# A two-layer decoder trunk: twelve instead of nine of 22 feed-forward groups in seven-product form, in a written order, with the weight sums kept in the loaded tiles

## The chip, the core and the metric

The kernel runs on one core of one Trainium2 chip. The metric is the device time of one execution in microseconds (us); less is better. The engines are named as in the profile: PE is TensorE (matmuls; PEld its weight loads), DVE is VectorE, ACT is ScalarE, POOL is GpSimd, SP is SyncE, which only issues DMAs here.

## What is computed

One sequence of 256 tokens with 2048 features passes a gated DeltaNet layer and an HGRN2 layer, each followed by a SwiGLU feed-forward part; all in float32.

```python
def swiglu(h, w_gate, w_up, w_down):
    return (jax.nn.silu(h @ w_gate) * (h @ w_up)) @ w_down

for layer in range(2):
    h = h + mixer[layer](rmsnorm(h, mixer_norm[layer]))
    h = h + swiglu(rmsnorm(h, ffn_norm[layer]), w_gate[layer], w_up[layer], w_down[layer])
return rmsnorm(h, final_norm)
```

w_gate and w_up are 2048 x 5632, w_down is 5632 x 2048. The change touches only the gate and up products of the two feed-forward parts.

## The kernel before

Every large weight is streamed once from HBM. The stream is a list of **items** (`stream`, L634). An item is one 128 x 1024 piece of a weight (512 KB). It is loaded by a DMA from SP's queue into a tile `raw` (a ring of four), then split in two: ACT copies it, rounded to fp32r, into `wh`, and DVE writes `wl` = raw - wh. Both have four buffers (SPLIT_BUFS). PE then makes three fp32r products in the place of one fp32 product: x_high with wh, x_high with wl, x_low with wh. So the split of an item can begin only when PE has finished the item four places before it, and a wl that comes late holds PE up.

The recording layer keeps the matmuls of the items in the order of the list. All other instructions are placed by a planner (`plan`, L319) with a table of costs and due times; it writes each engine's queue in a fixed order, and each engine executes its queue in that order. In the profile all instructions carry line 501, where the recorded queue is issued, so groups are told apart by the names of their tiles.

A feed-forward part has 22 **groups**, each of 256 gate and 256 up columns, and the `down` products in four parts that follow the groups 0-5, 6-11, 12-17 and 18-21. A group exists in two forms:

- plain (`gate_up`): eight items, each of 12 matmuls with 512 columns, all into one PSUM tile `main` (two of these, two banks each). ACT and DVE then make silu(gate) * up in two halves (`gated`).
- seven-product (`mixed_group`): the tokens, the contraction and the columns are halved, and seven products of half-size blocks replace eight (Strassen's scheme as Winograd wrote it). The sums of the activations are made once for each feed-forward part (`mix_inputs`, tiles `mixh`, `mixl`). The weights are taken in four **steps** (kk = 0 to 3). Each step loads two pieces, (b11, b12) and (b21, b22), into tiles `sraw` (a ring of four), and makes four items of them: b11 alone (product 1), then b21 and b22 (products 2 and 3), and two items of sums that DVE adds first, with two adds of 512 elements in each: (b11+b12, b22+b12) for products 5 and 7, and (b22+b11+b12, b22+b11+b12+b21) for products 6 and 4. The sums get `sraw` buffers of their own, so one step takes all four buffers. A step has 42 matmuls with 256 columns. The seven products lie in four PSUM banks, the `aux` tiles: 1 and 2 in the first, 3 and 7 in the second, 5 and 6 in the third, 4 in the fourth. There are only four `aux` banks, so the next such group begins when `end` has read the banks: ACT copies product 1 (`p1`), DVE makes v = product 6 - p1, then p1 + product 2, and so on through six more instructions.

FF_PLAN writes the order of the list. In "6 7 9 : 8 down 10 11 : 0000202..." the items of the seven-product groups 6, 7 and 9 are woven into those of groups 8, the waiting `down` part, 10 and 11: behind the k-th of these follow as many seven-product items as the k-th digit says.

Of the kernel before, what the change touches and what calls it, by code (L numbers as in the profile page):

```python
# [17 lines left out]
P = 128  # L18
T = 256
# [4 lines left out]
N_FF = 22  # L24
FF_PARTS = (6, 6, 6, 4)
FF_PLAN = (
# [4 lines left out]
)  # L31
N_HGRN = 4
LEVELS = (64, 32, 16, 8, 4, 2, 1)
# [491 lines left out]
class Trunk:  # L525
# [359 lines left out]
    def ffn(self, j, after):  # L885
# [68 lines left out]
        def mixed_group(gi):  # L954

            banks, raws = [], {}
# [21 lines left out]
            def raw_ring():  # L978
                return self.tile(self.pool, [P, 1024], "sraw", bufs=4, ordered=True)

            def add(out, x, y):
                nc.vector.tensor_tensor(out=out, in0=x, in1=y, op=ALU.add)

            def keep(half):
                def pre(raw):
                    raws[half] = quarters(raw)
                return pre

            def sums(which):
                def pre(t):  # L990
                    t = t.rearrange("p (n k c) -> p n k c", n=2, k=2)
                    (b11, b12), (b21, b22) = ([q[:, i] for i in range(2)] for q in (raws[0], raws[1]))
# [7 lines left out]
                return pre  # L1000

            def item(kk, src, pre, parts, part=None):
# [44 lines left out]
            for kk in range(4):  # L1047
                halves = [gu[gi, (kk + 4 * h) // 2][:, kk % 2 * 1024 : (kk % 2 + 1) * 1024] for h in range(2)]
                items += [
                    item(kk, halves[0], keep(0), [(1, lambda k: k * 512)], lambda x: quarters(x)[:, 0]),  # L1050
                    item(kk, halves[1], keep(1), [(2, lambda k: k * 512), (3, lambda k: k * 512 + T)]),
                    item(kk, None, sums(0), [(5, lambda k: k * T), (7, lambda k: 512 + k * T)]),
                    item(kk, None, sums(1), [(6, lambda k: k * T), (4, lambda k: 512 + k * T)]),
                ]
            items[0].begin, items[-1].end = begin, end
            return items
# [970 lines left out]
```

## Time and profile before

| what | value |
|---|---|
| time, median of 3 runs (lowest to highest) | 2727.85 us (2725.13 to 2728.78) |
| the profiled execution: its time, its span | 2727.04 us, 2725.3 us |
| PE, DVE, ACT busy, share of the span | 99 %, 78 %, 58 % |
| matmuls of seven-product groups, first and last | 870.0 to 1458.5 us, 2059.5 to 2648.0 us |
| HBM traffic over the span | 220 GB/s |

The profile shows one execution. Its page gives busy times by engine, the span in 40 slices, the chain of work that ended last, and the costliest groups of instructions; further views of the same trace give a timeline of single instructions, busy times in chosen windows, and who waited for whom. A row "out<-in" names the tile that is written and those that are read, with the buffer numbers left out. Two things have to be kept apart in it: the length of an instruction's row, and the time from its start to the start of the next one on the same engine, which can be less.

### The profile page before, as it was taken

Reading aid. Unit: us, or ns where it says so; the run is one execution under the profiler, and the core shown is the slowest. Engines: PE = TensorE matmul, PEld = TensorE weight load, DVE = VectorE, ACT = ScalarE, POOL = GpSimd, SP = SyncE. Lnnn points to the kernel's source line nnn. Section 1 sums busy time; section 2 is a strip of 40 time slices with the busy share of each in tenths; the row PEclk is TensorE's granted clock in tenths of the full one; section 3 lists DMA queues with packets and bytes.
Section 4 is the critical chain, followed back from the end, with each engine's and each line's share of the span. In section 5 each row is a group of like instructions: output and inputs, shape, how many; then the busy total and the mean of one; then the engine's idle time right before and its main releaser. Section 6 shows DMA issues by size and latency. Waiting matters only on the chain.

```text
span 2725.3 us, 44609 instructions
## 1 busy us (share of the span) xinstructions
PE 2707.2 (99%) x16966; PEld 2354.3 (86%) x16966; DVE 2129.8 (78%) x3221; ACT 1591.7 (58%) x2246; POOL 325.2 (12%) x466
## 2 busy tenths in 40 slices
PE   9999999999999999999999999999999999999998
PEld 9888888888888888888888989989888888888886
DVE  6887888787659778788788688678578788878786
ACT  7647676765555555565555656556465555555554
POOL 1222223222110000000000100000100000000010
PEclk9999999999999999999999999999999999999999
DMA  8686667687786677767777655545776777677775
GB/s 276 203 270 207 206 214 239 218 254 203 225 250 211 218 229 228 240 213 236 243 221 223 229 167 178 175 158 182 200 259 210 227 221 235 222 224 232 231 231 194
DMA packets 173959, 599.64 MB, mean 220 GB/s; under 512 B 21674, under 2 KB 22842, under 8 KB 173616
## 3 DMA queue, kind: packets, MB, share of 16 engines
q1 hardware_dynamic: 138912, 503.15, 55.8%
q0 software_dynamic: 34544, 92.79, 13.5%
q8 instruction: 133, 2.18, 0.3%
q10 hardware_dynamic: 288, 0.85, 0.1%
q14 instruction: 82, 0.67, 0.1%
HBM read 550.52 MB, written 48.28 MB: 220 GB/s over the span
## 4 chain that ended last, share of the span: by engine, by line
PE 97%; DVE 1%; ACT 1%; DMA 1%; issue 0%; SPq 0%; POOLq 0%; POOL 0%; ACTq 0%; DVEq 0%
PE main L501 78%; PE aux L501 19%; DVE turned L501 0%; ACT dec L501 0%; DVE wl L501 0%; DMA raw<-in_ffn_gu 0%; DMA first<-in_x 0%; ACT wh L501 0%; ACT xt_h L501 0%; ACT junk L501 0%; DVE htl L501 0%; DVE h L501 0%; SPq L501 0%; DVE p L501 0%; ACT mixh L501 0%
## 5 line engine op out<-in xcount | busy, mean ns | idle before, releaser
L501 ACT ACTIVATE wh<-raw 128x1024 fp32r<-128x1024 f32 x801 | 846.8, 1060 | 842.5 <-PE main L501 720.0
L501 DVE TENSOR_TENSOR wl<-raw,wh 128x1024 fp32r<-128x1024 f32 x801 | 982.7, 1229 | 421.2 <-ACT wh L501 413.5
L501 PE MATMUL main<-wl,xt_h 128*128 128x512 f32 x1600 | 626.8, 392 | 1.9 <-DVE wl L501 1.9
L501 PE MATMUL main<-wh,xt_h 128*128 128x512 f32 x1600 | 625.9, 391 | 1.2 <-ACT wh L501 1.2
L501 PE MATMUL main<-wh,xt_l 128*128 128x512 f32 x1600 | 625.7, 391 | 0.0
L501 DVE TENSOR_TENSOR wl<-sraw,wh 128x1024 fp32r<-128x1024 f32 (+1 forms) x288 | 308.0, 1087 | 65.9 <-ACT wh L501 64.8
L501 ACT ACTIVATE wh<-sraw 128x1024 fp32r<-128x1024 f32 (+1 forms) x288 | 271.8, 949 | 148.0 <-PE main L501 77.6
L501 PEld LDWEIGHTS main<-wh,xt_l 128*128 128x128 f32 x1600 | 300.7, 188 | 62.3
L501 PEld LDWEIGHTS main<-wl,xt_h 128*128 128x128 f32 x1600 | 300.6, 188 | 61.5 <-DVE wl L501 2.5
L501 PEld LDWEIGHTS main<-wh,xt_h 128*128 128x128 f32 x1600 | 300.5, 188 | 61.6 <-ACT wh L501 2.1
L501 PE MATMUL main<-xt_h,wh 128*128 128x256 f32 (+1 forms) x1040 | 289.1, 278 | 0.0
L501 PE MATMUL main<-xt_l,wh 128*128 128x256 f32 (+1 forms) x1040 | 288.5, 277 | 0.6 <-DVE xt_l L501 0.6
L501 PE MATMUL main<-xt_h,wl 128*128 128x256 f32 (+1 forms) x1040 | 288.0, 277 | 0.0
L501 PE MATMUL main<-wh,hth 128*128 128x512 f32 x688 | 268.9, 391 | 0.6 <-ACT hth L501 0.6
L501 PE MATMUL main<-wl,hth 128*128 128x512 f32 x688 | 268.9, 391 | 0.1
L501 PE MATMUL main<-wh,htl 128*128 128x512 f32 x688 | 268.1, 390 | 0.2
L501 PE MATMUL aux<-wl,mixh 128*128 128x256 f32 x864 | 239.2, 277 | 0.0
L501 PE MATMUL aux<-wh,mixh 128*128 128x256 f32 x864 | 239.2, 277 | 0.0
L501 PE MATMUL aux<-wh,mixl 128*128 128x256 f32 x864 | 239.1, 277 | 0.0
L501 PEld LDWEIGHTS main<-xt_l,wh 128*128 128x128 f32 (+1 forms) x1040 | 194.4, 187 | 1.3 <-DVE xt_l L501 0.8
L501 PEld LDWEIGHTS main<-xt_h,wh 128*128 128x128 f32 (+1 forms) x1040 | 194.4, 187 | 0.9
L501 PEld LDWEIGHTS main<-xt_h,wl 128*128 128x128 f32 (+1 forms) x1040 | 194.4, 187 | 0.0
(241 smaller groups left out, 3948.7 us busy)
## 6 DMA issues: line engine op xcount, KB each, us to landing
raw<-in_ffn_gu SPq DMA_DIRECT2D x208, 512.0 KB, 4.7
raw<-in_ffn_d SPq DMA_DIRECT2D x176, 512.0 KB, 4.8
sraw<-in_ffn_gu SPq DMA_DIRECT2D x144, 512.0 KB, 5.7
raw<-in_hgrn_in SPq DMA_DIRECT2D x128, 512.0 KB, 4.3
raw<-in_gdn_kq SPq DMA_DIRECT2D x64, 512.0 KB, 5.3
raw<-in_gdn_v SPq DMA_DIRECT2D x64, 512.0 KB, 4.5
raw<-in_gdn_z SPq DMA_DIRECT2D x64, 512.0 KB, 5.2
raw<-in_gdn_out SPq DMA_DIRECT2D x64, 512.0 KB, 5.3
```

The lines of the kernel that those rows point to most:

```text
L501: getattr(getattr(tc.nc, op.eng), op.method)(*args, **kw)
```

## The change

Twelve groups instead of nine take the seven-product form in each of the two feed-forward parts: groups 4, 11 and 17 are new. The order is written anew: a digit may now be 1 to 6, where it was 0 or 2. And the weight sums are written over the loaded pieces: b11+b12 over b11, b22+b12 over b12, b22+b11+b12 over b22, and the last sum over b21. So a step takes two of the four `sraw` buffers instead of all four, and the first add has to come behind the split of the first item, which reads b11.

```diff
-    "0 | 2 : 1 3 4 5 : 00000002002002002002002002002000",
-    "6 7 9 : 8 down 10 11 : 000020202202022020220202202022020220202202020000",
...
+    "0 | 2 4 : 1 3 5 : 000222022222022222022200",
+    "6 7 9 11 : 8 down 10 : 0213230124002250412010350050110402060002",
...
-                    if which == 0:
-                        raws[2] = t[:, 0]
-                        add(t[:, 0], b11, b12)
-                        add(t[:, 1], b22, b12)
-                    else:
-                        add(t[:, 0], b22, raws[2])
-                        add(t[:, 1], t[:, 0], b21)
+                    if which == 0:
+                        add(b11, b11, b12)
+                        add(b12, b22, b12)
+                    else:
+                        add(b22, b22, b11)
+                        add(b21, b22, b21)
...
-                return Item(src, mm, pre, ring=raw_ring, part=part)
+                return Item(src, mm, pre, ring=lambda: raws[half] if src is None else raw_ring(half), part=part)
...
-                    item(kk, None, sums(0), [(5, lambda k: k * T), (7, lambda k: 512 + k * T)]),
-                    item(kk, None, sums(1), [(6, lambda k: k * T), (4, lambda k: 512 + k * T)]),
+                    item(kk, None, 0, sums(0), [(5, lambda k: k * 512), (7, lambda k: k * 512 + T)]),
+                    item(kk, None, 1, sums(1), [(6, lambda k: k * 512 + T), (4, lambda k: k * 512)]),
```

**The first place is the change from group 6 to group 7** in the first feed-forward part. On PE stand, before, the last matmuls of group 6 (tile aux_1555, product 4) and what follows them, a `down` item:

```order
L501 MATMUL aux_1554_10217<-wl_1636_10598,mixh_1316_8895 128x256
L501 MATMUL aux_1554_10217<-wh_1635_10587,mixl_1317_8896 128x256
L501 MATMUL aux_1555_10241<-wh_1635_10587,mixh_1316_8895 128x256
L501 MATMUL aux_1555_10241<-wl_1636_10598,mixh_1316_8895 128x256
L501 MATMUL aux_1555_10241<-wh_1635_10587,mixl_1317_8896 128x256
L501 MATMUL main_1624_10535<-wh_1638_10605,hth_1515_8891 128x512
```

Two such items of 12 matmuls (5138 to 5161 in PE's order) lie there between the two groups. In the changed kernel group 7 follows group 6 at once, with product 1 in aux_1635:

```order
L501 MATMUL aux_1559_10261<-wh_1618_10584,mixh_1316_8895 128x256
L501 MATMUL aux_1559_10261<-wl_1619_10601,mixh_1316_8895 128x256
L501 MATMUL aux_1559_10261<-wh_1618_10584,mixl_1317_8896 128x256
L501 MATMUL aux_1560_10306<-wh_1618_10584,mixh_1316_8895 128x256
L501 MATMUL aux_1560_10306<-wl_1619_10601,mixh_1316_8895 128x256
L501 MATMUL aux_1560_10306<-wh_1618_10584,mixl_1317_8896 128x256
L501 MATMUL aux_1635_10649<-wh_1621_10596,xt_h0_12_68 128x256
L501 MATMUL aux_1635_10649<-wl_1622_10614,xt_h0_12_68 128x256
```

DVE's order at the same place, before: `p4` is v, and the row that reads aux_1552 is the last reader of group 6's first bank.

```order
L501 TENSOR_TENSOR wl_1642_10644<-raw_1640_10510,wh_1641_10627 128x1024
L501 TENSOR_TENSOR p4_1644_10658<-aux_1554_10217,p1_1643_10583 128x256
L501 SCALAR_TENSOR_TENSOR p1_1643_10583<-aux_1552_10147,rstd_3_59,p1_1643_10583 128x256
L501 TENSOR_TENSOR wl_1651_10669<-sraw_1649_10528,wh_1650_10646 128x2x256
L501 TENSOR_TENSOR sg_1646_10675<-aux_1554_10217,p4_1644_10658 128x256
L501 TENSOR_TENSOR wl_1654_10681<-sraw_1652_10550,wh_1653_10661 128x1024
L501 TENSOR_TENSOR h1_1645_10688<-aux_1553_10161,sg_1646_10675 128x2x256
L501 TENSOR_TENSOR p4_1644_10658<-aux_1553_10161,p4_1644_10658 128x256
L501 SCALAR_TENSOR_TENSOR p4_1644_10658<-aux_1555_10241,rstd_3_59,p4_1644_10658 128x256
```

And in the changed kernel, from the split of group 6's last item (wl_1619); aux_1557 is group 6's first bank:

```order
L501 TENSOR_TENSOR wl_1619_10601<-sraw_1609_10365,wh_1618_10584 128x1024
L501 TENSOR_TENSOR wl_1622_10614<-sraw_1620_10435,wh_1621_10596 128x2x256
L501 TENSOR_TENSOR sraw_1620_10435<-sraw_1620_10435 128x2x256
L501 TENSOR_TENSOR wl_1625_10632<-sraw_1623_10492,wh_1624_10609 128x1024
L501 TENSOR_TENSOR p4_1627_10642<-aux_1559_10261,p1_1626_10592 128x256
L501 SCALAR_TENSOR_TENSOR p1_1626_10592<-aux_1557_10209,rstd_3_59,p1_1626_10592 128x256
L501 TENSOR_TENSOR sg_1629_10647<-aux_1559_10261,p4_1627_10642 128x256
L501 TENSOR_TENSOR p4_1627_10642<-aux_1558_10225,p4_1627_10642 128x256
L501 TENSOR_TENSOR h1_1628_10657<-aux_1558_10225,sg_1629_10647 128x2x256
L501 TENSOR_TENSOR wl_1634_10666<-raw_1632_10464,wh_1633_10628 128x1024
```

What moved: the plain items between the two groups are gone, and five reads of the banks stand in one run, with three rows between them and the split of the last item. Groups 13 and 15 meet in the same way, so there are two such places in each feed-forward part. At six others one plain item (four places) or two (two places) lie between.

**The second place is where the first seven-product group begins**, group 2. DVE's order there before (wl_1372 is the split of its first item; turned, h1 and mixl belong to `mix_inputs`):

```order
L501 TENSOR_TENSOR h1_1325_9209<-turned_1323_9108,h1_1324_9176 128x512
L501 TENSOR_TENSOR mixl_1317_8896<-h1_1324_9176,mixh_1316_8895 128x512
L501 TENSOR_TENSOR wl_1372_9222<-sraw_1370_8883,wh_1371_9211 128x2x256
L501 TENSOR_TENSOR mixl_1317_8896<-h1_1324_9176,mixh_1316_8895 128x512
L501 TENSOR_TENSOR mixl_1317_8896<-h1_1325_9209,mixh_1316_8895 128x512
L501 SCALAR_TENSOR_TENSOR h1_1348_9238<-main_1326_8900,rstd_3_59,sg_1349_8881 128x256
L501 SCALAR_TENSOR_TENSOR h1_1348_9238<-main_1326_8900,rstd_3_59,sg_1350_8882 128x256
L501 TENSOR_TENSOR h1_1325_9209<-turned_1322_9090 128x512
L501 TENSOR_TENSOR wl_1375_9249<-sraw_1373_8884,wh_1374_9235 128x1024
L501 TENSOR_TENSOR mixl_1317_8896<-h1_1325_9209,mixh_1316_8895 128x512
L501 TENSOR_TENSOR wl_1385_9267<-raw_1383_9154,wh_1384_9256 128x1024
L501 TENSOR_TENSOR wl_1392_9296<-raw_1390_9169,wh_1391_9277 128x1024
```

And in the changed kernel (wl_1360 is the split of its first item):

```order
L501 TENSOR_TENSOR turned_1322_9115<-xt_h1_13_69,xt_l1_17_73 128x1024
L501 TENSOR_TENSOR wl_1357_9123<-raw_1355_9040,wh_1356_9102 128x1024
L501 TENSOR_TENSOR wl_1360_9132<-sraw_1358_8883,wh_1359_9126 128x2x256
L501 TENSOR_TENSOR sraw_1358_8883<-sraw_1358_8883 128x2x256
L501 TENSOR_TENSOR sraw_1358_8883<-sraw_1361_8884,sraw_1358_8883 128x2x256
L501 TENSOR_TENSOR turned_1323_9146<-xt_h3_15_71,xt_l3_19_75 128x1024
L501 TENSOR_TENSOR turned_1322_9115<-turned_1322_9115,rstd_row_9_65 128x1024
L501 TENSOR_TENSOR wl_1363_9162<-sraw_1361_8884,wh_1362_9148 128x1024
L501 TENSOR_TENSOR sraw_1361_8884<-sraw_1361_8884,sraw_1358_8883 128x2x256
L501 TENSOR_TENSOR wl_1366_9175<-raw_1364_9062,wh_1365_9165 128x1024
L501 TENSOR_TENSOR sraw_1361_8884<-sraw_1361_8884 128x2x256
L501 TENSOR_TENSOR turned_1323_9146<-turned_1323_9146,rstd_row_9_65 128x1024
```

What moved: the group begins 12 plain items behind the start of the feed-forward part instead of 16, and most of the rows of `mix_inputs` for the second half of the contraction (tiles 1322 and 1323) now stand among the rows of the group.

More of the change, by code (lines that the diff above doesn't have):

```diff
@@ L976, in quarters, with raw_ring, sums, pre @@
                 return ap.rearrange("p (k h c) -> p h k c", k=2, h=2)
-            def raw_ring():
-                return self.tile(self.pool, [P, 1024], "sraw", bufs=4, ordered=True)
+            def raw_ring(half):
+                raws[half] = self.tile(self.pool, [P, 1024], "sraw", bufs=4, ordered=True)
+                return raws[half]
             def add(out, x, y):
                 nc.vector.tensor_tensor(out=out, in0=x, in1=y, op=ALU.add)
-            def keep(half):
-                def pre(raw):
-                    raws[half] = quarters(raw)
-                return pre
[L989 to L992, printed above, removed]
-                    if which == 0:
-                        raws[2] = t[:, 0]
-                        add(t[:, 0], b11, b12)
-                        add(t[:, 1], b22, b12)
-                    else:
-                        add(t[:, 0], b22, raws[2])
-                        add(t[:, 1], t[:, 0], b21)
-                return pre
-            def item(kk, src, pre, parts, part=None):
+            def sums(which):
+                def pre(_):
+                    (b11, b12), (b21, b22) = ([quarters(r)[:, i] for i in range(2)] for r in (raws[0], raws[1]))
+                    if which == 0:
[4 more added lines that the diff above has]
+                        add(b21, b22, b21)
+                return pre
+            def item(kk, src, half, pre, parts, part=None):
                 def mm(wh, wl):
@@ L1049, in mixed_group @@
                 items += [
-                    item(kk, halves[0], keep(0), [(1, lambda k: k * 512)], lambda x: quarters(x)[:, 0]),
-                    item(kk, halves[1], keep(1), [(2, lambda k: k * 512), (3, lambda k: k * 512 + T)]),
-                    item(kk, None, sums(0), [(5, lambda k: k * T), (7, lambda k: 512 + k * T)]),
-                    item(kk, None, sums(1), [(6, lambda k: k * T), (4, lambda k: 512 + k * T)]),
+                    item(kk, halves[0], 0, None, [(1, lambda k: k * 512)], lambda x: quarters(x)[:, 0]),
+                    item(kk, halves[1], 1, None, [(2, lambda k: k * 512), (3, lambda k: k * 512 + T)]),
+                    item(kk, None, 0, sums(0), [(5, lambda k: k * 512), (7, lambda k: k * 512 + T)]),
+                    item(kk, None, 1, sums(1), [(6, lambda k: k * 512 + T), (4, lambda k: k * 512)]),
                 ]
```

4 rows, old and new, of the table FF_PLAN are left out of this document.

## The prediction

> **What bounds the kernel now.** The first part of the page gives the busy time of each engine, its share of the span and its instructions; the fourth gives the chain that ended last.
>
> ```profile
> span 2725.3 us, 44609 instructions
> PE   2707.2 (99%) x16966; PEld 2354.3 (86%) x16966; DVE 2129.8 (78%) x3221; ACT 1591.7 (58%) x2246; POOL 325.2 (12%) x466
> PE 97%; DVE 1%; ACT 1%; DMA 1%; issue 0%; SPq 0%; POOLq 0%; POOL 0%; ACTq 0%; DVEq 0%
> ```
>
> PE is busy 99% of the span and is 97% of the chain. So time is won only by giving PE fewer matmul columns, and lost wherever another engine then makes it wait. The view of waits has what PE waited for, with total us, times and the longest:
>
> ```profile
> PE main L501 <- DVE wl L501: 1.9, 2, 0.9
> PE main L501 <- ACT wh L501: 1.2, 2, 1.1
> ```
>
> In 2725 us PE waited four times for a split weight, 3.1 us in all. The next question is how near DVE, which makes the weight sums and the low halves, is to its limit in the feed-forward parts. The windows have the length, then busy us and instructions of PE, PEld, DVE, ACT and POOL, the granted clock, the DMA share and GB/s. The first is the entry of the first feed-forward part, the others its woven middle.
>
> ```profile
> 840.00:860.00 20.00, 20.00 (x90) 16.57 (x89) 20.00 (x23) 11.50 (x15) 0.00 (x0) 1.00 0.57 189
> 1060.00:1100.00 40.00, 40.00 (x239) 35.42 (x238) 34.20 (x45) 23.09 (x26) 2.19 (x3) 1.00 0.83 245
> 1100.00:1140.00 40.00, 40.00 (x231) 35.17 (x230) 33.74 (x43) 22.81 (x26) 2.22 (x4) 1.00 0.66 216
> ```
>
> DVE has no free time at the entry, where it makes the activation sums, and 5.8 to 6.3 us of 40 in the middle. ACT has 17. So DVE decides whether PE stays fed, and what the change adds to DVE has to be set against these 15%.
>
> **What one instruction costs.** For PE the starts in the timeline count (start, length of the row, group), not the lengths, since matmuls overlap. This is the end of one seven-product group, one plain item, and the start of the next group.
>
> ```profile
> 1399.94 0.28 PE L501 MATMUL aux<-wh,mixl 128*128 128x256 f32 x1
> ...
> 1400.96 0.28 PE L501 MATMUL aux<-wh,mixl 128*128 128x256 f32 x1
> 1401.07 0.40 PE L501 MATMUL main<-wh,hth 128*128 128x512 f32 x1
> ...
> 1403.82 0.28 PE L501 MATMUL aux<-wh,xt_h 128*128 128x256 f32 x1
> ...
> 1404.53 0.28 PE L501 MATMUL aux<-wh,mixh 128*128 128x256 f32 x1
> ...
> 1405.90 0.40 PE L501 MATMUL main<-wh,hth 128*128 128x512 f32 x1
> ```
>
> The 12 matmuls of a plain item take 2.75 us (1401.07 to 1403.82), or 0.229 each. The six of product 1 take 0.71, or 0.118 each; the 12 after them take 1.37, or 0.114 each. For DVE the same care is needed:
>
> ```profile
> 849.86 1.22 DVE L501 TENSOR_TENSOR wl<-raw,wh 128x1024 fp32r<-128x1024 f32 x1
> 851.00 2.36 DVE L501 TENSOR_TENSOR turned<-turned,rstd_row 128x1024 f32<-128x1024 f32 x2
> 853.27 1.23 DVE L501 TENSOR_TENSOR wl<-raw,wh 128x1024 fp32r<-128x1024 f32 x1
> ...
> 856.17 1.29 DVE L501 TENSOR_TENSOR mixl<-h,mixh 128x512 fp32r<-128x512 f32 x2
> 857.38 0.69 DVE L501 TENSOR_TENSOR h<-turned,turned 128x512 f32<-128x512 f32 x1
> 857.98 1.22 DVE L501 TENSOR_TENSOR wl<-raw,wh 128x1024 fp32r<-128x1024 f32 x1
> ```
>
> Rows of 1.22 us start 1.135 apart (851.00 to 853.27 holds two), rows of 0.69 us start 0.60 apart (857.38 to 857.98). The two at 851.00 write the tile that they read, and are no slower: sums written over the raw tile cost what sums in a tile of their own cost. The end of the same group on DVE:
>
> ```profile
> 1400.93 0.42 DVE L501 TENSOR_TENSOR p<-aux,p 128x256 f32<-128x256 f32 x1 [0.59 <-PE aux L501]
> 1401.39 0.49 DVE L501 SCALAR_TENSOR_TENSOR p<-aux,rstd,p 128x256 f32<-128x256 f32 x1
> 1401.79 1.22 DVE L501 TENSOR_TENSOR wl<-sraw,wh 128x1024 fp32r<-128x1024 f32 x1
> 1402.92 0.42 DVE L501 TENSOR_TENSOR sg<-aux,p 128x256 f32<-128x256 f32 x1
> 1403.38 0.42 DVE L501 TENSOR_TENSOR p<-aux,p 128x256 f32<-128x256 f32 x1
> 1403.72 0.68 DVE L501 TENSOR_TENSOR h<-aux,sg 128x512 f32<-128x512 f32 x1
> ```
>
> Rows of 256 elements cost 0.34 (1403.38 to 1403.72) and 0.40 (1401.39 to 1401.79).
>
> **The change, part by part.**
>
> *PE's work.* A plain group is 96 matmuls of 512 columns, 96 x 0.229 = 22.0 us. A seven-product group is 24 x 0.118 + 144 x 0.114 = 19.25 us. Three groups in each of two feed-forward parts: 6 x 2.7 = **-16.3 us**. PE gives this back only where it waits.
>
> *DVE's work.* A plain group costs it 8 x 1.135 + 2 x 0.40 = 9.9 us. A seven-product group has, in each of four steps, one split of half size, three whole ones and four adds, 3 x 1.135 + 5 x 0.60 = 6.4, and 3.1 us of reads at its end (five rows at 0.34, two at 0.40, one at 0.60): 28.7. So DVE gets 6 x 18.8 = 113 us more. It has the room on the whole, but not everywhere. I counted its rows and PE's matmuls in the changed order from the split of group 2's first item over 219 items, up to the second place where two such groups meet. DVE: 195 rows of 1024, 187 of 512, 40 + 30 + 27 small ones (the last are transposes, estimated at 0.34 like other rows of 256), or 195 x 1.135 + 187 x 0.60 + 35 = 368 us. PE: 1416 x 0.114 + 1008 x 0.229 = 392 us. That is 94%, and three places in it are over 100%.
>
> *Wait 1, the entry.* Over the first 17 items of group 2's stretch DVE has 19 rows of 1024, 22 of 512 and 3 of 256: 36.0 us (11 of the 44 rows are what is left of the activation sums). PE needs 114 x 0.114 + 72 x 0.229 = 29.5 us. DVE falls back by 6.5 us. Its lead is limited by the four buffers: a split starts when PE ends the item four before, three items of 2.75 us are then left, and a copy on ACT (1060 ns in the page's row) and the split (1.22) go off:
>
> ```profile
> L501 ACT ACTIVATE wh<-raw 128x1024 fp32r<-128x1024 f32 x801 | 846.8, 1060 | 842.5 <-PE main L501 720.0
> ```
>
> 8.25 - 2.3 = at most 5.9, some 5.6 with the hops between engines. I take 1.0 us of waiting; with the smaller lead that can be read here,
>
> ```profile
> 866.00 1.22 DVE L501 TENSOR_TENSOR wl<-sraw,wh 128x1024 fp32r<-128x1024 f32 x1
> 870.83 0.28 PE L501 MATMUL aux<-wl,mixh 128*128 128x256 f32 x1
> ```
>
> 3.6 us, it would be 2.9, and with a little more lead nothing. Twice: **+2.0** (0 to 5.8).
>
> *Wait 2, where two groups meet without an item between.* The new group's first matmul needs a bank that DVE frees with the second read of the old group. In the rows above that read ends at 1401.88, while PE's next matmul started at 1401.07: with no plain item PE would have waited 0.9. That is the least. If DVE comes with no lead, the three rows that now stand ahead of the reads (0.60 + 0.60 + 1.135) and the two reads (0.9) leave 3.2 us against the 1.4 us of the last item, a wait of 1.9. Four such places, between 3.6 and 7.6; I take 1.3 each, as half of them are met with a full lead: **+5.2**. The other six changes of group in each part have at least one plain item, and the rows above show that such an item covers it: the next group began at 1403.82 without a pause, though the last read of the old one was not done.
>
> *Wait 3, behind the second such place.* In its ten items DVE has 22.1 us of rows and PE 16.4 of matmuls. Some 3 us of lead and 1.7 of the wait itself leave **+2.0** for the two parts (0 to 4).
>
> *Loads.* The 48 loads of the six groups go from the ring of `raw` to that of `sraw`; their number is the same. DVE's adds waited little for them,
>
> ```profile
> DVE sraw L501 <- DMA sraw<-in_ffn_gu: 2.2, 3, 1.5
> sraw<-in_ffn_gu SPq DMA_DIRECT2D x144, 512.0 KB, 5.7
> ```
>
> 2.2 us in the middle of the first part (980 to 1460 us), against a landing time of 5.7. A step now frees two buffers for two loads while the next step has its own two, so a load may start a whole step (4.8 us of PE at least, mostly 8 or more) earlier. I cost it at nothing; without that cover it would be the 2.2 us in each part, grown by 12/9, some 6 in all, most of it hidden by DVE's lead.
>
> *Sum:* -16.3 + 2.0 + 5.2 + 2.0 = -7.1. The profiled execution took 2727.04 us, 1.7 more than its span and 0.8 less than the median; on the median this gives 2727.85 - 7.1 = **2720.7 us**.
>
> **The rivals.**
>
> *Nearly all hidden.* If DVE has its full lead at the entry and the places of meeting cost the least: -16.3 + 3.6 = **2715**. For it: in the profile not one wait for the feed-forward splits exceeds 1.1 us. Against it: DVE's 20.00 of 20 at the entry.
>
> *DVE becomes the bound (slower).* If in the dense stretch a row costs DVE its whole length, because neighbours wait for each other or for ACT's copies, the 219 items cost 195 x 1.22 + 187 x 0.69 + 42 = 409 us against PE's 392. Less 5.6 of lead, 12 us of waiting in each part, the places of meeting in it: -16.3 + 24 = **2736**. It decides from 8 us in each part on, that is from about 1.175 us for a row of 1024. For it: in the middle of the first part (980 to 1460 us) DVE's splits do wait for ACT again and again.
>
> ```profile
> DVE wl L501 <- ACT wh L501: 83.4, 81, 1.5
> ```
>
> Against it: those waits come when DVE is ahead, and where it is behind (849 to 860) the rows stand at 1.135.
>
> [...]
>
> *The banks come free later (no change).* In the rows above a split stands between the reads, and the read `h` of the second bank ends 3.4 us behind the group's last matmul. If the new group needs that bank for product 3, 1.05 us behind its start, it waits 2.3 at each place, and the splits queued behind the reads come later by as much: 9.2 and some 3 us more in place of 5.2: -16.3 + 2.0 + 9.2 + 3 + 2.0 = -0.1, **2727.7**. Against it: the changed order has the five reads in one run.
>
> **How the numbers follow.** Forecast (2717 to 2725) 0.5; hidden 0.14; the banks 0.2; DVE the bound 0.16. The range leaves out the far halves of the first and the last: 2712 to 2734. A measurement tells about 0.2% (5.5 us) from no change, so faster is below 2722.4: of the forecast 0.40, all of the hidden case, and 0.03 of the banks, 0.57. Slower is above 2733.3: 0.13 of the last rival. The rest, 0.30, is the same.
>
> **What would show it.** Right: matmul rows of products 2 to 7 (`aux` from `mixh`) 1152 of each kind instead of 864; PE's waits for DVE `wl` some 4 us and for DVE `p` some 5; four pauses of 1 to 2 us where `aux` follows `aux`; DVE near 39 of 40 us in the windows behind the entry. Wrong: DVE rows of 1024 in that stretch starting 1.2 apart; waits for `mixl`, for DMA or for ACT's copies that the sum has at nothing; more than 8 us of pauses in one feed-forward part.

## The result and the profile after

The changed kernel takes 2732.32 us, the median of 14 runs (2729.57 to 2736.30); the kernel before, in the same sessions, takes 2726.59 (2724.66 to 2728.78). The ratio is 1.0023, with a 95% interval of 1.0016 to 1.0030. The change costs 5.7 us where 7.1 were forecast to be won: slower, by just over what can be told from no change. The profiled execution took 2735.53 us, 3.2 above the median, with a span of 2733.8; against the 2725.3 before, 8.5 us are to be explained.

The page of the changed kernel, its parts 1 and 4:

```profile
span 2733.8 us, 45721 instructions
PE 2700.2 (99%) x17398; PEld 2364.8 (87%) x17398; DVE 2253.2 (82%) x3401; ACT 1630.8 (60%) x2300; POOL 325.1 (12%) x466
PE 88%; DVE 6%; DMA 2%; issue 2%; ACT 1%; POOL 0%; SPq 0%; POOLq 0%; ACTq 0%; DVEq 0%
```

PE is busy 7.0 us less than before, and DVE 123 us more. But the chain that ended last, which was PE for 97%, is PE for only 88%, with 6% on DVE and 2% on a DMA. So other work now ends last. What PE waited for, over the whole span (total us, times, longest):

```profile
PE aux L501 <- DVE p L501: 5.6, 4, 1.6
PE aux L501 <- DVE wl L501: 5.2, 10, 1.1
PE main L501 <- DVE wl L501: 3.3, 4, 0.9
...
PE aux L501 <- ACT wh L501: 2.3, 2, 1.6
PE main L501 <- ACT hth L501: 1.2, 1, 1.2
```

The first row has exactly four entries, the four meetings of groups. The other rows are not all from where the prediction looked. This view takes a pause from the end of the row before, and rows of matmuls overlap (rows of 0.28 us start 0.114 apart); so the pauses are better read from starts. In the two feed-forward parts I took every matmul and counted what its start comes later than 0.1137 us (256 columns) or 0.2275 us (512) behind the start before it, where that is over 0.03. The sum is 0.6 and 0.1 us before, 11.4 and 10.3 after. By place, in both parts together:

| place (us in the profile) | forecast | found |
|---|---|---|
| entry: 889.7, 2083.4 | 2.0 | 1.6 |
| four meetings: 1006.0, 1244.5, 2198.0, 2436.4 | 5.2 | 6.9 |
| DVE around the second meeting: 1241, 1262, 1304, 2433, 2454, 2497 | 2.0 | 3.6 |
| 999.3 to 1004.7, 1287, 2192, 2479.9 | 0 | 9.3 |
| elsewhere | | 0.3 |

The last but one row is the surprise. The chain over 985 to 1010 us (start, length, what) tells what happened at its largest place:

```profile
985.00 12.13 DMA turned<-blocks_home
997.15 0.04 ACTq L501
997.19 0.05 issue
997.24 1.07 ACT hth L501
998.32 1.23 DVE htl L501
999.55 1.15 DVE wl L501
...
1000.74 4.17 PE aux L501 x20
```

A finished pair of groups (here 4 and 5, the third pair) is transposed on its way through HBM: POOL stores it (`blocks_home`) and reads it back (`turned`), ACT copies it into `hth`, DVE makes `htl`. The last of its four DMAs took 12.13 us. ACT's queue is fixed, and `hth` stood in it ahead of two copies `wh`; so ACT stood still, then DVE, then PE. ACT's waits in the first part have a row that is not there before:

```profile
ACT hth L501 <- DMA turned<-blocks_home: 9.4, 3, 5.7
```

What PE did then (start, length of the row, and in brackets the idle time and what ended it):

```profile
999.29 0.38 PE L501 MATMUL aux<-wh,mixh 128*128 128x256 f32 x1 [1.63 <-ACT wh L501]
1000.74 0.39 PE L501 MATMUL aux<-wl,mixh 128*128 128x256 f32 x1 [1.07 <-DVE wl L501]
...
1001.60 0.42 PE L501 MATMUL aux<-wh,mixh 128*128 128x256 f32 x1
1001.81 0.41 PE L501 MATMUL aux<-wl,mixh 128*128 128x256 f32 x1
```

Two pauses, 1.79 and 1.33 us by the starts, and behind them matmuls that start 0.21 apart instead of 0.114. The windows (length, busy us and instructions of PE, PEld, DVE, ACT, POOL, granted clock, DMA share, GB/s) show why, and the last two answer to those of before:

```profile
990.00:995.00 5.00, 5.00 (x33) 4.46 (x33) 4.29 (x6) 1.49 (x3) 0.00 (x0) 1.00 1.01 261
995.00:1000.00 5.00, 3.04 (x13) 2.05 (x11) 1.68 (x2) 2.77 (x3) 0.00 (x0) 1.00 0.27 104
1000.00:1005.00 5.00, 4.26 (x23) 4.26 (x23) 4.32 (x6) 3.07 (x5) 0.00 (x0) 0.66 0.52 179
...
1060.00:1100.00 40.00, 40.00 (x249) 35.88 (x248) 37.40 (x47) 23.94 (x26) 4.01 (x6) 1.00 0.89 253
1100.00:1140.00 40.00, 40.00 (x246) 35.78 (x245) 36.58 (x44) 23.51 (x26) 4.00 (x6) 1.00 0.78 246
```

From 990 to 995 all DMA engines are busy (1.01). From 995 to 1000 their share is 0.27, and PE (3.04 of 5), DVE (1.68) and ACT (2.77) stand still for much of the time: they wait for one block, directly or through ACT's queue. From 1000 to 1005 the granted clock is 0.66 on the mean, and 0.50 from 1001.5 to 1004.5. In the dense windows DVE is at 36.6 to 37.4 of 40, full but not over. The DMA issues over 975 to 1000 us of the changed kernel (count, size, median us from issue to landing):

```profile
raw<-in_ffn_d SPq DMA_DIRECT2D x5, 512.0 KB, 7.3
sraw<-in_ffn_gu SPq DMA_DIRECT2D x2, 512.0 KB, 8.5
...
turned<-blocks_home POOLq DMA_DIRECT2D x4, 128.0 KB, 11.5
```

and over 965 to 990 us of the kernel before, around the same block:

```profile
raw<-in_ffn_d SPq DMA_DIRECT2D x6, 512.0 KB, 4.6
sraw<-in_ffn_gu SPq DMA_DIRECT2D x3, 512.0 KB, 6.1
...
turned<-blocks_home POOLq DMA_DIRECT2D x4, 128.0 KB, 3.0
```

All that is under way at that time lands late, the loads on SP's queue (7.3 us against 4.6 and 8.5 against 6.1) as well as the block on POOL's (11.5 against 3.0).

### The profile page after: what moved, and what is told of

The parts are those of the page before. It is cut to its first block, busy times and chain, and to the rows that moved or that the text cites. A ratio compares the mean times of both kernels' runs of the same rounds, so it can differ in the third digit from the quotient of the medians.

```text
span 2733.8 us, 45721 instructions
## 1 busy us (share of the span) xinstructions
PE 2700.2 (99%) x17398; PEld 2364.8 (87%) x17398; DVE 2253.2 (82%) x3401; ACT 1630.8 (60%) x2300; POOL 325.1 (12%) x466
## 4 chain that ended last, share of the span: by engine, by line
PE 88%; DVE 6%; DMA 2%; issue 2%; ACT 1%; POOL 0%; SPq 0%; POOLq 0%; ACTq 0%; DVEq 0%
PE main L501 68%; PE aux L501 19%; DVE wl L501 3%; DMA turned<-blocks_home 2%; DVE sraw L501 1%; DVE turned L501 1%; DMA raw<-in_ffn_gu 1%; ACT wh L501 1%; ACT dec L501 0%; DVE h L501 0%; DMA first<-in_x 0%; POOL turned L501 0%; DVE htl L501 0%; DVE p L501 0%; ACT hth L501 0%
## 5 line engine op out<-in xcount | busy, mean ns | idle before, releaser
L501 PE MATMUL main<-wl,xt_h 128*128 128x512 f32 x1408 | 552.0, 392 | 1.9 <-DVE wl L501 1.9
L501 PE MATMUL main<-wh,xt_l 128*128 128x512 f32 x1408 | 550.8, 391 | 0.0
L501 ACT ACTIVATE wh<-sraw 128x1024 fp32r<-128x1024 f32 (+1 forms) x384 | 362.5, 951 | 314.7 <-PE main L501 146.4
L501 DVE TENSOR_TENSOR wl<-sraw,wh 128x1024 fp32r<-128x1024 f32 (+1 forms) x384 | 411.9, 1085 | 58.0 <-ACT wh L501 55.4
L501 PE MATMUL aux<-wl,mixh 128*128 128x256 f32 x1152 | 320.8, 278 | 5.2 <-DVE wl L501 5.2
L501 PE MATMUL aux<-wh,mixh 128*128 128x256 f32 x1152 | 319.8, 278 | 2.3 <-ACT wh L501 2.3
L501 PE MATMUL aux<-wh,mixl 128*128 128x256 f32 x1152 | 319.6, 277 | 0.0
L501 PEld LDWEIGHTS aux<-wl,mixh 128*128 128x128 f32 x1152 | 217.0, 188 | 11.1 <-DVE wl L501 7.1
L501 PEld LDWEIGHTS aux<-wh,mixh 128*128 128x128 f32 x1152 | 217.3, 189 | 7.3 <-ACT wh L501 3.2
L501 PEld LDWEIGHTS aux<-wh,mixl 128*128 128x128 f32 x1152 | 217.2, 189 | 0.0
```

The source lines that it names most:

```text
L501: getattr(getattr(tc.nc, op.eng), op.method)(*args, **kw)
```

## The experiments

Theory A: the loss comes from turned blocks that land late and stand in front of weights in ACT's queue, and beside them from the meetings and from DVE's length at a few places. Its rivals: B, DVE is simply the bound; C, the sums in place cost; F, which came up on the way, twelve groups leave a shortage that moves on wherever a place is relieved; D and G stand with their runs. Each kernel was timed beside the kernel before. "Pauses" are those of the two feed-forward parts, counted as above.

| run | time, us | ratio to before (95%) | pauses, us |
|---|---|---|---|
| e1_sums | 2727.03 | 1.0002 (0.9994 to 1.0011) | 0.5 + 0.1 |
| e2_order | 2755.40 | 1.0105 (1.0089 to 1.0120) | 19.3 + 22.3 |
| e3_turn12 | 2737.66 | 1.0040 (1.0027 to 1.0052) | 11.2 + 11.8 |
| e4_apart | 2724.28 | 0.9992 (0.9984 to 1.0001) | 4.7 + 5.7 |
| e5_late2 | 2731.51 | 1.0015 (1.0006 to 1.0024) | 12.5 + 9.2 |
| e6_add_out | 2724.54 | 0.9994 (0.9986 to 1.0003) | 5.6 + 5.0 |
| e7_group4 | 2724.27 | 0.9992 (0.9983 to 1.0001) | 1.8 + 1.0 |
| e9_thin | 2730.46 | 1.0017 (1.0008 to 1.0026) | 8.0 + 7.0 |
| e10_late26 | 2724.38 | 0.9996 (0.9987 to 1.0005) | 7.1 + 5.2 |
| e11_apart26 | 2723.26 | 0.9993 (0.9984 to 1.0002) | 4.7 + 5.7 |
| e12_more | 2728.82 | 1.0011 (1.0002 to 1.0020) | 8.1 + 7.0 |
| e13_ring3 | 2804.92 | 1.0293 (1.0278 to 1.0307) | 44.2 + 49.2 |
| e14_more6 | 2718.74 | 0.9971 (0.9959 to 0.9983) | 2.2 + 3.1 |

The kernel before took 2726.63 or 2726.58 us beside the runs up to e9_thin, 2725.33 beside e10_late26 to e13_ring3 and 2726.27 beside e14_more6. So runs of different rows are better compared by their ratios. The counts of pauses end at the same two times in every run. In e1_sums, e4_apart, e6_add_out, e7_group4, e10_late26, e11_apart26 and e14_more6, as in the kernel before, the first number therefore holds 0.4 us of a pause at the end of the part that the others have a little later, and the 3.1 of e14_more6 holds 1.4 us of the same kind; like for like e14_more6 has 1.8 and 1.7.

An edit makes the planner write all queues anew. So a run can differ from the changed kernel in more places than the one that the edit aims at.

### The two halves of the change

e1_sums: the changed code with the order of before.

```diff
-    "0 | 2 4 : 1 3 5 : 000222022222022222022200",
+    "0 | 2 : 1 3 4 5 : 00000002002002002002002002002000",
```

(and the other three strings of before).

> The nine groups and the order of before, with the sums written over the loaded tiles. PE's work is that of before. Theory A (the loss came from transfers of a turned block that land late, and from places where two groups meet; the sums cost nothing themselves): 2726.6 plus or minus 2, DVE rows of 512 elements still 0.60 apart, no wait of ACT for a turned tile. Rival C (the sums in place, with the first add behind the split, are what costs): at least a third of the 21.9 us of waits, so 2730 or more.

2727.03, no change, and no pause that was not there before. The sums in place are free; rival C falls.

e2_order: the code of before with the order of the change, so with sums in buffers of their own.

> The twelve groups and the order of the change, with the sums in buffers of their own as before, so that a step again takes all four buffers of sraw. Theory A: the freed buffers let loads run ahead in bursts that hold up the turned block; with the old ring the bursts are smaller and the transfer of the turned block lands within 9 us, but a dense step has to wait for its own loads, a landing time of 5.7 us behind the last split of the step before, some 1 to 3 us for each step that follows another without a pause: slower than the changed kernel, 2735 to 2760, with waits of DVE for sraw of 20 us or more. Rival C (the sums in place cost): below the changed kernel's 2732.3, near 2720.

2755.4. The waits of DVE and of ACT in the first part:

```profile
DVE sraw L501 <- DMA sraw<-in_ffn_gu: 21.6, 16, 3.6
ACT wh L501 <- DMA sraw<-in_ffn_gu: 30.3, 16, 4.7
```

That is what A said: sixteen times a step waits for its own loads. So for this order the freed buffers are worth 23 us, and the two halves of the change belong together. The turned block did not hold ACT up in this run.

### The late block

e3_turn12: the planner is told of a longer landing time, for all blocks.

```diff
-LANDING_OF = {"wide": 7.0, "u": 7.0}
+LANDING_OF = {"wide": 7.0, "u": 7.0, "turned": 12.0}
```

> The changed kernel, but the planner is told that the transfer of a turned block lands after 12 us instead of 6.5, so hth and htl stand some five places later in the queues of ACT and DVE. Theory A: ACT's waits for turned (9.4 us in the first feed-forward part) go to under 2, PE's pauses at 999 to 1005 (5.0 us, half clock included) and at 2192 (2.3) and 2480 (1.3) go for the most part: 6 to 9 us less, 2723 to 2726.5, with no half clock at 1001. Rival B (DVE is simply too full, and the late block only took time that would have been lost a little later): the pauses come back within the next 20 us, 2730 to 2733.

2737.66, a miss of both. The pauses at 999, 1287, 2192 and 2480 are gone, but at 1196 and 2389 PE itself now waits for the sixth block's `hth`, which stands too late: 4.3 us by `hth` and `htl`, and with the slower matmuls behind them (granted clock 0.69 from 1196 to 1201, 0.52 from 2389 to 2394) 6.2 and 6.7 of the pauses in the two parts.

e5_late2: the longer landing time for the third block alone.

```diff
             t = self.turn_through(h1s[pair])
+            if pair == 2:
+                for op in nc.ops[-4:]:
+                    op.lag = 12.0
```

> The changed kernel, in which only the copy hth of the third turned block (groups 4 and 5) and its htl stand about five places later in the queues of ACT and DVE, once in each feed-forward part; all else is in the order of the changed kernel. Theory A (the block that lands late holds up the copies of weights queued behind it on ACT, and PE with them): the pauses at 999 to 1005 (5.0 us with the half clock) and at 2192 to 2193 (2.3) go and nothing takes their place: 6 to 7.5 us less than the changed kernel, 2725 to 2726.5; no stretch of half clock. Rival B (DVE is full there anyway): at least half comes back as waits for wl before 1030, 2729 to 2732.

2731.51. The pauses at 999 and 2192 are gone, as A said, and nothing came back before 1030. But then the seventh block (groups 12 and 13) held ACT up, in the first part by

```profile
ACT hth L501 <- DMA turned<-blocks_home: 6.0, 1, 6.0
```

and PE waited 2.7 us for a `wh` behind it.

The time lies in B's range, but not for B's reason, since what came back is the wait for another block, 280 us later. Is it one mechanism in two places, or a shortage that moves on? e10_late26 has the same edit with `if pair in (2, 6)`.

> The changed kernel with the copies hth of the third and of the seventh turned block (groups 4 and 5, 12 and 13) some five places later on ACT, in each feed-forward part. Moving the third alone took the pauses at 999 to 1005 away, but the seventh block then held ACT for 6.0 us and PE paused at 1287. Theory A (both are one mechanism, a late block in front of weights on ACT): only the entry, the meetings and what lies around the second meeting are left, some 5.3 us in each part against the 10.3 to 11.4 of the changed kernel: 2720 to 2725.5. Rival F (the pauses come from a shortage that moves on to the next block or to wl whenever one place is relieved): 2729 to 2733 again.

2724.38: 7.9 us less than the changed kernel (7.4 by the ratios), inside A's range, outside F's. ACT has no wait for a block left in either part, and PE's waits in the first part are down to

```profile
PE aux L501 <- DVE p L501: 2.4, 2, 1.6
PE aux L501 <- DVE wl L501: 1.1, 3, 0.5
```

The pauses fell from 21.7 to 12.3, or by 9.8 like for like, where the table by place has 9.3 for the late blocks.

e13_ring3 asks why the block is late. `bufs=4` of the ring of `sraw` becomes `bufs=3`.

> The changed kernel with three buffers of sraw instead of four, so that only one load of the next step can run ahead. It tells why the block lands late. Theory A (loads that run ahead fill the 16 DMA engines while the block is under way): its second leg lands within 9 us everywhere and ACT waits for it less than 2 us in all, as with the old ring, but steps that follow each other wait for the second load, 5.7 us of landing behind a split, some 1 to 2 us at 10 to 20 places in each part: 2740 to 2765. Rival G (the block is late by the place in POOL's queue alone): the waits for the turned block stay at 8 to 9 us in each part.

2804.92, far more than A's 2740 to 2765, since steps wait for loads much longer:

```profile
ACT wh L501 <- DMA sraw<-in_ffn_gu: 38.2, 18, 4.9
```

ACT waits for no turned block, and the longest landing of a block, as the median of its four DMAs, is 8.4 us (11.5 in the changed kernel, 7.5 before). That speaks against G, and so does the chain above, where the time lies behind POOL's issue. But with 73 us more than the changed kernel for the same bytes the DMA engines also have more time, so this run is weak evidence for the cause that A gives.

The traces of the two kernels show more. While the third block is under way, from POOL's issue to the landing, SP's queue (q1) moves this much (packets, MB, share of the 16 DMA engines), over 974 to 979 us before and over 983 to 997 us in the changed kernel:

```profile
q1 hardware_dynamic: 98, 0.38, 26.0%
```

```profile
q1 hardware_dynamic: 781, 2.82, 70.8%
```

In the changed kernel SP issues five loads of 512 KB from 980.6 to 985.8, two for `sraw` and three for `raw`; before, it issues none between 970.9 and 976.1. So the block shares the engines with a burst of loads (from 990 to 995 its queue, q0, has 24.3% of the time of the 16 engines, and q1 has 75.0%), and most of them are not those of `sraw`. The seventh block has another neighbour, from POOL's own queue: a store of 512 KB that POOL issues 0.7 us ahead of it, and 17 us ahead before (1273.15 and 1290.53).

```profile
1272.12 1.17 POOL L501 DMA_DIRECT2D x_home<-x  x1 [6.30 <-ACT wh L501]
1272.84 2.69 POOL L501 DMA_DIRECT2D turned<-blocks_home  x4
```

Nor is the landing the whole of it. POOL's issue of the third block and ACT's copy of it, before and in the changed kernel:

```profile
974.01 2.18 POOL L501 DMA_DIRECT2D turned<-blocks_home  x4 [6.72 <-DMA blocks_home<-turned]
987.35 1.04 ACT L501 ACTIVATE hth<-turned 128x1024 fp32r<-128x1024 f32 x1
```

```profile
983.37 2.18 POOL L501 DMA_DIRECT2D turned<-blocks_home  x4 [6.93 <-ACT wh L501]
997.24 1.06 ACT L501 ACTIVATE hth<-turned 128x1024 fp32r<-128x1024 f32 x1 [5.75 <-DMA turned<-blocks_home]
```

Before, ACT came to the copy 13.3 us behind the first issue, and the block had landed after 4.7. In the changed kernel ACT came after 8.1 us and the block landed after 13.8. The new order had moved both. Either half of the change alone makes this block late as well: its four DMAs take 7.8 and 6.8 us (median, first and second part) in e1_sums, 6.4 and 7.5 in e2_order, against 3.0 before and 11.5 and 9.9 in the changed kernel. But there ACT comes to the copy 11 to 16 us behind the issue, and does not wait.

### The meetings and DVE

e4_apart: one plain item or two between the groups.

```diff
-    "6 7 9 11 : 8 down 10 : 0213230124002250412010350050110402060002",
-    "12 13 15 17 : 14 down 16 : 1012330220212020400532060400310140314200",
+    "6 7 9 11 : 8 down 10 : 0213230122202250412010350050110402060002",
+    "12 13 15 17 : 14 down 16 : 1012330220212020400523060400310140314200",
```

> The changed kernel with three digits of the order moved in the second and the third part, so that one plain item or two lie between groups 6 and 7 and between 13 and 15. Theory A: the four pauses at the meetings (6.6 us) go, and some of the 5.7 us around the second of them: 6 to 10 us less, 2722 to 2726. The late turned block stays where it is. Rival B (DVE is the bound over the stretch): only the 6.6 move to other places, 2730 to 2733.

2724.28, 8.0 us less than the changed kernel, as A said. The four pauses at the meetings are gone. A pause of 2.4 us for `wl` behind group 13 has come in each part, and the blocks' waits are smaller here without being aimed at (3.7 us on ACT in the first part instead of 9.4).

e6_add_out takes DVE's load down.

```diff
                         add(b11, b11, b12)
-                        add(b12, b22, b12)
```

> Leaves out one of the four adds of each step, b22+b12, so that products 7 and 4 are not those of the reference; it takes 96 x 0.60 = 58 us from DVE and nothing from PE. Theory A (two causes: the late block 8.6 us, and DVE's own length at the entry, at the meetings and around the second of them 13.9): the entry pauses (1.6), those around the second meeting (5.7) and about half of the four meetings (6.6) go, the late block stays: 7 to 11 us less, 2721 to 2725. Rival B (DVE is the whole cause): also the pauses at 999 and 2192 go, 16 us or more less, below 2717. Rival D (DVE's length plays no part): within 3 us of the changed kernel.

2724.54, in A's range, but not for all of A's reasons. The pauses at the entry and around the second meeting are gone, and those of the late blocks too (ACT has no wait for a block in the first part), which A did not say: ACT comes to the third block's copy 12.2 us behind the issue here, where the changed kernel has 8.1; a new one of 1.4 us for `wl` stands at 1324 and 2512. The meetings stayed. DVE at the second meeting, in the changed kernel,

```profile
1241.22 1.22 DVE L501 TENSOR_TENSOR wl<-raw,wh 128x1024 fp32r<-128x1024 f32 x1
1242.35 1.22 DVE L501 TENSOR_TENSOR wl<-sraw,wh 128x1024 fp32r<-128x1024 f32 x1
1243.49 0.42 DVE L501 TENSOR_TENSOR p<-aux,p 128x256 f32<-128x256 f32 x1
```

and with one add less in each step,

```profile
1236.54 1.23 DVE L501 TENSOR_TENSOR wl<-raw,wh 128x1024 fp32r<-128x1024 f32 x1 [0.21 <-ACT wh L501]
1237.92 1.23 DVE L501 TENSOR_TENSOR wl<-sraw,wh 128x1024 fp32r<-128x1024 f32 x1
1239.06 0.42 DVE L501 TENSOR_TENSOR p<-aux,p 128x256 f32<-128x256 f32 x1
```

where the copy on ACT for the second of these splits is

```profile
1236.82 1.06 ACT L501 ACTIVATE wh<-sraw 128x1024 fp32r<-128x1024 f32 x1 [0.31 <-PE aux L501]
```

Here DVE has time to wait for ACT, so it is not behind, and yet the pause is 2.12 us (1.76 in the changed kernel) and the one at the first meeting 0.95 in both. The last split of the old group stands in front of the reads; it needs a copy of ACT, and that copy waited for PE, which frees the buffer. In the changed kernel DVE's rows stand there without a gap, so DVE binds it; with less on DVE this chain binds it in its place, and the pause is no shorter. Rival D falls by the entry, and B by the meetings.

e7_group4: only the first of the four strings is that of the change, ten groups in all.

> Only the first part of the order of the change (groups 2 and 4 woven into 1, 3 and 5), the other three as before, all with the sums in place: ten groups of seven products in each feed-forward part. PE's work is 2 x 2.7 = 5.4 us less than before. No place where two groups meet. Theory A: the entry costs its 1.6 us, the late third block up to 3 in each part if it is again in front of weights on ACT: 2723 to 2727 (2722.8 if the block does not hurt). Rival B (DVE's length decides): the entry and the end of the part wait 4 us or more in each part for wl, slower than 2729.

2724.27, as A said: 2.8 us of pauses, 1.6 of them at the entry. The gain to be had by 5.2 us less of PE's work (two groups by 2.58, see below) is half used up.

e9_thin: as e4_apart, with the third block's copy later and the densest digits spread.

```diff
-    "12 13 15 17 : 14 down 16 : 1012330220212020400523060400310140314200",
+    "12 13 15 17 : 14 down 16 : 1012330220212020410423150400310140314200",
```

> The change with plain items between the groups (as in the run with three digits moved), the copy of the third turned block five places later, and in the third part the densest digits spread, 4 1 0 4 2 3 1 5 for 4 0 0 5 2 3 0 6. Theory A: against the run with three digits moved (2724.3) the late block in the second feed-forward part (1.4 us) and most of the 2.5 us of wl waits at the densest place in each part go: 2718 to 2721. Rival B: the waits for wl only move, 2723 to 2725.

2730.46, a miss of all. The pause behind group 13 was as long as before (2.4 us), so it is not one of density; that it comes from the five reads at the group's end is likely, since e12_more, with plain items there, has no such pause. The seventh block was late again (ACT waits 2.9 and 3.1 us), and new pauses came at 1285, 1302, 2448, 2474 and 2491.

e11_apart26: e4_apart with the edit of e10_late26.

> Both remedies: plain items between groups 6 and 7, 13 and 15, and the third and the seventh block's copies later on ACT. The run with plain items alone had 4.7 and 5.7 us of pauses in the two parts, of which 1.4 at 2184 by the third block and some 2.4 in each part behind group 13. Theory A: 1.5 to 2 us less than that run's 2724.3, 2721 to 2724. Rival F: a new pause of 3 us or more by another block, 2726 or more.

2723.26, in A's range, but by the ratios (0.9993 and 0.9992) no faster than e4_apart, and its pauses are those of e4_apart (10.4). The two remedies do not add up, since in e4_apart the blocks cost little.

### A version that beats both

e12_more: e11_apart26 with two changes of the order.

```diff
-    "0 | 2 4 : 1 3 5 : 000222022222022222022200",
+    "0 | 2 4 : 1 3 5 : 000022202222202222202220",
...
-    "12 13 15 17 : 14 down 16 : 1012330220212020400523060400310140314200",
+    "12 13 15 17 : 14 down 16 : 1012330220212020400520305050310140314200",
```

> As the run before, and two more changes of the order: the first group of seven products begins one plain item later (000022202222202222202220), and two plain items lie behind group 13 (520305050 for 523060400). Theory A with the sizes read so far: the entry pause (0.8 in each part) and the one behind group 13 (2.4) go: 4 to 6 us less than the run before, 2716 to 2720, below before by more than its spread. Rival F: pauses of wl come back elsewhere, 2722 or more.

2728.82, a miss. The pauses at the entry and behind group 13 are gone, as A said; but groups 4 and 5 now end later, and the copy that was moved back for them comes too late for the `down` items. PE's waits in the first part, and ACT's row:

```profile
PE main L501 <- ACT hth L501: 3.1, 1, 3.1
...
```

```profile
1010.06 1.04 ACT L501 ACTIVATE hth<-turned 128x1024 fp32r<-128x1024 f32 x1
```

e14_more6 is the same with `if pair == 6`: the third copy stands three places earlier on ACT.

> The run with more changes of the order (2728.8), but the third block's copy hth is left where the planner puts it by itself, three places earlier on ACT; the seventh's stays moved. That run had no pause left at the entry nor behind group 13, and 15.1 us of pauses in all, of which 10.8 in two places (1011 and 2201) where PE waited for a hth that stood too late, half-clock matmuls behind it included. Theory A (the place of hth in ACT's queue against the landing of the block is what decides, too early holds up weights, too late holds up the down items): these 10.8 us go, 2717 to 2721, faster than before by 0.2% or more. Rival F (a shortage that moves on): at least half comes back, 2723 or more.

2718.74, and the kernel before 2726.27 beside it: ratio 0.9971 (0.9959 to 0.9983), faster than both kernels. ACT's row, and PE's only wait left in the first part:

```profile
1005.94 1.04 ACT L501 ACTIVATE hth<-turned 128x1024 fp32r<-128x1024 f32 x1
```

```profile
PE aux L501 <- DVE wl L501: 0.6, 2, 0.4
```

Three places in one queue are 10 us of 2719. The chain on its page, beside that of the changed kernel above:

```profile
PE 95%; DVE 3%; ACT 1%; issue 1%; DMA 1%; SPq 0%; POOLq 0%; POOL 0%; DVEq 0%; ACTq 0%
```

With the same 17398 matmuls and 3401 instructions of DVE, the chain is PE's again. Rival F falls: twelve groups leave no shortage that must come back.

## Why the prediction was wrong

**PE's work, -16.3: found about -14.1.** The span of e10_late26 is 1.3 us under that of before; its pauses in the two parts are 11.6 more and those elsewhere 1.2 more, so the work is 1.3 + 11.6 + 1.2 = 14.1 less. The changed kernel gives 13.7 in the same way, e4_apart 14.3, e14_more6 14.2. The term was taken from two short stretches, 0.229 for a matmul of 512 columns; the mean spacing over a whole part is 0.2276, and 0.1147 for 256. (6 x 2.7 is also 16.2, not 16.3.) Then a plain group is 96 x 0.2276 = 21.85, a seven-product group 168 x 0.1147 = 19.27, and the gain 6 x 2.58 = 15.5. Of the 1.4 us that are left, 1.0 is the mean spacing of the 3400 wide matmuls, which is 0.0003 longer in the changed kernel.

**Wait 1, the entry, +2.0: right**, 1.6, at `wl` of the group's second step. e6_add_out (less for DVE to do) and e12_more (a later start) took it away. The 0.3 us of hops that the prediction takes off the lead stand in no row that it shows; the trace of before has 0.28 at one place of the entry, where ACT's copy at 867.53 starts 0.25 behind PE's first matmul of the next item (867.28) and DVE's split at 868.62 starts 0.03 behind the end of that copy.

**Wait 2, the meetings, +5.2: right in kind and nearly in size**, 6.9, inside the 3.6 to 7.6 (the least, 0.9, is 0.81 by the rows that it shows, 1401.88 less 1401.07; found 0.95), and 5.4 by the first late starts of e10_late26, where nothing else disturbs them. That DVE's lead decides between 0.9 and 1.9 was not right: with DVE unloaded the pauses stayed (0.95 and 2.12).

**Wait 3, behind the second meeting, +2.0: found 3.6**, at the upper end of its bounds (4); 1.2 of it lies ahead of the meeting.

**Loads, "I cost it at nothing": this is the step that failed**, 9.3 us. The question that it asked was whether DVE would wait for its `sraw`, and the answer was right: those waits went from 2.2 us to none. What it left out is that loads which start earlier and closer together meet other transfers (SP's queue had 70.8% of the DMA engines' time beside the third block, 26.0% before), and that the new order also moves the copy `hth` that waits for one of them. The cover of the block was not named: before, every copy `hth` came up when its block had landed, with landings of 3.0 to 7.5 us; now they are 3.0 to 11.5. For the third block the cover was 13.3 - 4.7 = 8.6 us; the order took 5.2 of it by the earlier turn on ACT, and the landing came 9.1 later. By these numbers, as an estimate, neither would have held ACT up for more than 0.5 us alone. The prediction listed "waits for DMA that the sum has at nothing" as what would make it wrong, but no rival had that price, and the range held the time only because it reached far for another reason.

**The rivals.** DVE as the bound did not happen: its rows of 1.22 us start 1.13 apart at the second meeting (1241.22, 1242.35, 1243.49). The banks were free as forecast, not later.

The sum with what was found is -14.1 + 1.6 + 6.9 + 3.6 + 9.3, with 0.3 elsewhere in the parts less the 0.7 that was there before, and 1.2 outside: 8.1, against 8.5 of the spans. The median lies 3.2 under the profiled execution. Its runs spread over 6.7 us (before 4.1), as one would expect if the late blocks differ from run to run; that was not measured.

What stays open: how much of the block's delay each of its neighbours causes, and whether another queue for it would help; that was not tried.

## What to carry to other kernels

A copy that waits for a DMA holds up all that is queued behind it on its engine (here ACT stood 5.75 us, and PE then 1.79 and 1.33), so its place in the queue is a bet on the landing time: ask for every such copy how many us lie between the issue and its turn, and what a few us more would stop. A new order moves that turn as well as the landing. When a change frees buffers, loads can start earlier; price what that does to the other transfers under way (in e1_sums, where nothing but the sums is new, the third block took 7.8 and 6.8 us in place of 3.0), not only to the loads. A remedy at one such place has to be measured with the others: here one block moved back gained 0.8 us, two gained 7.9, and one that stood three places too late lost 10.

## What the hardware showed

PE's clock fell behind short pauses, and not behind all of them. The window 1000 to 1005 above has a mean clock of 0.66, and from 1001.5 to 1004.5 the clock is 0.50; at 0.50 that is 5 x 0.34 / 0.5 = 3.4 us of the window, and it followed two pauses of 1.79 and 1.33 us with a matmul between. It cost about 1.6 us more. Shorter pauses did it now and then: behind group 13 e4_apart, e9_thin and e11_apart26 have the same 2.4 us in both parts. In two of the six cases the clock fell (to a mean of 0.66 from 1245 to 1250 in e9_thin and of 0.72 from 2430 to 2436 in e11_apart26); in the windows of the other four it is 1.00. The window behind it in e9_thin, and in e4_apart:

```profile
1245.00:1250.00 5.00, 4.75 (x19) 4.08 (x20) 4.96 (x8) 1.66 (x2) 0.00 (x0) 0.66 0.87 292
```

```profile
1243.00:1248.00 5.00, 4.84 (x27) 4.23 (x28) 4.96 (x9) 1.59 (x2) 0.00 (x0) 1.00 0.81 270
```

What tells the two cases from the four is not shown.

And the same kind of block, 512 KB read back by four DMAs from POOL's queue, took 3.0 to 11.5 us from issue to landing (median of the four) in one execution, that of the changed kernel. Beside the slowest, over 983 to 997 us, SP's queue moved 2.82 MB (70.8% of the 16 DMA engines' time); beside one of 3.0 us, over 1352.4 to 1356.5, it moved 0.02 MB (1.0%).
